# A decoder layer in split float32: two activation tiles start 224 bytes further on

## The chip, the core and the metric

One core of one Trainium2 chip runs the whole layer as one program. The metric is the device time of that program in microseconds (us), the median of the runs shown. Lower is better. Engines are named as in the profile: PE (TensorE, matmul), PEld (its weight loads), DVE (VectorE), ACT (ScalarE), POOL (GpSimd), SP (SyncE, which issues nearly all DMAs here).

## The reference, cut to what matters

The layer works on 256 tokens of width 2048, all float32, batch 1:

```
x = x + 0.5 * swiglu(rms_norm(x), ffn1)                 # 2048 -> 5632 (gate, up) -> 2048
h = rms_norm(x);  proj = h @ w_in                       # 2048 -> 11776
#   dilated attention (3 groups x 4 heads of 128), differential attention (4 heads of 2 x 128), two gates
y = sigmoid(gA) * (o_dil @ w_dil) + sigmoid(gB) * (o_diff @ w_diff)
x = x + y @ w_out
x = x + 0.5 * swiglu(rms_norm(x), ffn2)
```

Per-head norms of queries and keys, a partial rotary embedding and the softmaxes stand between; nearly all arithmetic is in the products with the weight matrices.

## The kernel before, in words

**A product in three parts.** Each weight matrix is read once, 512 columns (a chunk) by 256 rows (a group, two k tiles) at a time. `weight_groups` loads a group into `raw` (4 buffers), ACT rounds it into `w_hi` (line 94, float32r), DVE writes the rest `w_lo = raw - w_hi` (line 95); both have 3 buffers. The activations were split the same way into a high and a low tile, feature on the partitions: `xh`/`xl` for the input of the feed-forwards and of `w_in`, `ah`/`al` for the hidden layer, `oa_h`/`oa_l` and `ob_h`/`ob_l` for the two attention outputs, `yh`/`yl` for the input of `w_out`. `linear` then issues three matmuls per k tile and token tile, 12 per group:

```
nc.tensor.matmul(ps[t], xh[:, k, sl], hi[:, kk], start=k == 0, stop=False)       # line 110
nc.tensor.matmul(ps[t], xh[:, k, sl], lo[:, kk], start=False, stop=False)        # line 111
nc.tensor.matmul(ps[t], xl[:, k, sl], hi[:, kk], start=False, stop=k == nk - 1)  # line 112
```

The activation block of 128 x 128 is the operand that is loaded into the array (stationary), the 512 weight columns are streamed (moving). The names `xh, xl` inside `linear` are its parameters; the profile shows the tile that was passed.

**Stages.** First feed-forward (gate and up chunks in turn with `xh`/`xl`, then the down product with `ah`/`al`), the mixer (`w_in` with `xh`/`xl`, attention heads in between), four rounds of a gate chunk (`xh`/`xl`), a dilated branch chunk (`oa_h`/`oa_l`, 24 matmuls) and a differential branch chunk (`ob_h`/`ob_l`, 48 matmuls), then `w_out` (`yh`/`yl`), and the second feed-forward as the first. `xh`/`xl` serve 6432 of the 9216 big matmuls: 2144 on each of the three lines.

**Transposes through DRAM.** The hidden layer comes out with tokens on the partitions. `turn_blocks` transposes 32 x 32 blocks on DVE (line 154), writes them to DRAM (`blocks`, line 156) and reads them back in place (`moved`, line 159), both on SP's queue. `split_blocks` makes `ah`/`al` of it (lines 127 and 128), emitted 8 groups later (`BLOCK_WAIT`), so that PE has matrix products in front of it. ACT and DVE work in order: while ACT waits for `moved`, the next `w_hi` behind it waits too.

**Order.** The order on each engine was set when the program was built, by a scheduler; on the chip each engine keeps it and waits on semaphores. `masks` (line 282) builds the attention masks from an index table `DI` that POOL writes with an iota (line 286), and a helper table `DM`; `rsqrt_mean` (line 121) runs a power on POOL for each norm. `junk` is a work tile of one buffer that takes results which nobody reads.

**Where the tiles lie.** The built program places them at these byte addresses of a partition; the last column is the address modulo 512. Inside every one of these tiles the operands of a matmul start at multiples of 512 bytes from the tile's start.

| tile | start, before | modulo 512 |
|---|---|---|
| xh, xl | 33472, 49856 | 192 |
| w_hi (3 buffers) | 94112, 98208, 102304 | 416 |
| w_lo (3 buffers) | 106400, 110496, 114592 | 416 |
| ah, al | 120736, 165792 | 416 |
| oa_h, oa_l, ob_h, ob_l | 120736 to 137120 | 416 |
| yh, yl | 145312, 161696 | 416 |
| ident; xs | 32896; 16512 | 128 |
| dk, dq, dv, at | 161696 to 192416 | 416 |
| fq, fk, fv | 204768 to 221152 | 480 |

Of the kernel before, what the change touches and what calls it, by code (L numbers as in the profile page):

```python
# [11 lines left out]
F32 = mybir.dt.float32  # L12
F32R = mybir.dt.float32r
I32 = mybir.dt.int32
# [5 lines left out]
P = 128  # L20
NT = 2            # token tiles
S = P * NT
# [3 lines left out]
KF = FF // P  # L26
CH = 512          # columns of one weight chunk
BLOCK_WAIT = 8    # weight groups a transpose through DRAM is given
GRP = 2           # k tiles of one weight load and split
DIL_G, DIL_H = 3, 4  # L30
# [9 lines left out]
    '0x1.fa8b84p-14', '0x1.be2188p-15', '0x1.88ec22p-16', '0x1.5a0f4ep-17', '0x1.30c94ep-18')]  # L40
# 2*pi in parts whose products with a turn count below 2**19 are exact
TWO_PI = (6.25, 17.0 / 512.0, -19.0 * 2.0 ** -20)
# [5 lines left out]
def hybrid_layer_kernel(ctx: ExitStack, tc: tile.TileContext, a: dict, out: bass.AP):  # L48
# [11 lines left out]

# [1 line left out]
    # Work that hangs on ACT and DVE is emitted some weight groups later, so that the tensor engine has  # L62
    # matrix products in front of it while it waits.
    groups = 0
# [17 lines left out]
    def weight_groups(w, n0, nk):  # L82
        """Weight columns n0..n0+CH, GRP k tiles at a time, as exact float32r parts."""
        nonlocal last_hi, last_lo
        for k0 in range(0, nk, GRP):
            raw = wraw.tile([P, GRP, CH], F32, name="raw")
            hi = wspl.tile([P, GRP, CH], F32R, name="w_hi")
            lo = wspl.tile([P, GRP, CH], F32R, name="w_lo")
            step = 1 if groups == 0 else GRP
            for g in range(0, GRP, step):  # L90
                ks = slice(g, g + step)
                nc.sync.dma_start(raw[:, ks], w[(k0 + g) * P:(k0 + g + step) * P, n0:n0 + CH]
                                  .rearrange("(k p) n -> p k n", p=P))
                last_hi = nc.scalar.activation(hi[:, ks], raw[:, ks], AF.Copy)  # L94
                last_lo = nc.vector.tensor_tensor(lo[:, ks], raw[:, ks], hi[:, ks].bitcast(F32), op=ALU.subtract)  # L95
            yield k0, hi, lo

    def linear(w, n0, xh, xl, nk, ahead=None):
        """x @ w[:, n0:n0+CH] for both token tiles, left in PSUM."""
        ps = [ps_mm.tile([P, CH], F32, name="mm") for _ in range(NT)]  # L100
# [15 lines left out]
    def rsqrt_mean(ss, n, cols):  # L116
        """(ss / n + eps) ** -0.5 on [P, cols]"""
        v = small.tile([P, cols], F32, name=f"rv{cols}")
# [5 lines left out]
    def split(hi, lo, src, gain=None):  # L124
        """hi + lo = src (times a per-partition gain)"""
        if gain is None:
# [6 lines left out]
    def to_kmajor(srcs, xh, xl, k0, gains=None):  # L133
        """srcs: per token tile [P, m * 2 * P]; fills xh/xl[:, k0:k0+2*m, :] with the split transpose."""
        for h in range(srcs[0].shape[-1] // (2 * P)):
# [12 lines left out]
    def turn_blocks(srcs, pool, x=None):  # L148
        """The transpose of srcs (per token tile [P, CH]) without the tensor engine: blocks of 32 x 32
        on DVE, then a trip through DRAM that brings the blocks to their partitions.  # L150
        Block row a holds tokens 32 a + j, feature 128 kt + 4 i + q goes to partition 4 i + q of k tile kt."""
        r = pool.tile([P, 4, NT, 4, 32], F32, name="turned")               # (a i) | q t kt j
        for t in range(NT):
            nc.vector.transpose(r[:, :, t], srcs[t].rearrange("p (kt i q) -> p q kt i", i=32, q=4))  # L154
        d = dram.tile([4, P, NT * P], F32, name="blocks")                  # a | (i q) | t kt j
        nc.sync.dma_start(d.rearrange("a (i q) x -> (a i) q x", q=4), r.rearrange("p q t kt j -> p q (t kt j)"))
        if x is None:
            x = pool.tile([P, 4, NT, 4, 32], F32, name="moved")            # (i q) | a t kt j
        nc.sync.dma_start(x.rearrange("p a t kt j -> p a (t kt j)"), d.rearrange("a p x -> p a x"))
        return x  # L160

    def split_blocks(x, xh, xl, k0, gains=None):
        """xh/xl[:, k0:k0+4, :] from turn_blocks"""
        for t in range(NT):
# [16 lines left out]

# [1 line left out]
    xs = const.tile([P, NT, D], F32, name="xs")           # residual stream, tokens on partitions  # L183
    xv = a["x"][0].rearrange("(t p) d -> p t d", p=P)
# [4 lines left out]
    table = const.tile([P, 1], F32, name="table")  # L189
    nc.scalar.activation(table, mhalf[:, :1], AF.Silu)    # loads the table of the feed-forward  # L190

    def gain_columns(names, name):
        """Gains as columns of [P, number of 128-blocks]"""
        n = sum(a[k].shape[1] for k in names) // P
# [11 lines left out]

    xh = const.tile([P, KD, S], F32R, name="xh")          # feature-major operand of the linear layers
    xl = const.tile([P, KD, S], F32R, name="xl")
    g1 = gain_columns(["ffn1_norm"], "g1")

    def load_x(i):
        """256 columns of x, and their transpose"""
        if i < KD // 2:
# [37 lines left out]
    def residual(n, ps, scale, gains, ss, pool):  # L251
        """x += scale * ps on columns of chunk n; starts the next norm."""
        cols = slice(n * CH, (n + 1) * CH)
# [18 lines left out]

# [1 line left out]
    H = ROPE // 2  # L274
# [7 lines left out]
    def masks():  # L282
        # masks: 0 where a key counts, NEG elsewhere; queries of the second token tile, keys 0..255
        # (its second half is also the mask of the first tile's own keys)
        di = const.tile([P, P], I32, name="DI")                # query - key inside a tile
        nc.gpsimd.iota(di, pattern=[[-1, P]], base=0, channel_multiplier=1)
        nc.vector.tensor_scalar(mask[:, 0, P:], di, 0.0, None, op0=ALU.is_lt)
        nc.vector.tensor_scalar(mask[:, 0, :P], di, 0.0, None, op0=ALU.is_gt)
        dm = const.tile([P, P], I32, name="DM")
        for g, r in ((1, 4), (2, 16)):  # L290
# [7 lines left out]
    def rotary():  # L298
        # rotary tables, per token: [cos | cos] and [-sin | sin]
        pos = const.tile([P, NT], I32, name="pos")  # L300
# [29 lines left out]
    def head_gains():  # L330
        # q/k gains on every partition, and lambda
        for i, n in enumerate(("dil_q_norm", "dil_k_norm", "diff_q_norm", "diff_k_norm")):
# [11 lines left out]

# [1 line left out]
    later_gains = []  # L346
# [9 lines left out]
    def pinned(fn):  # L356
        """fn, behind the splits traced so far on ACT and DVE"""
        with tc.issue_after(last_hi.ins), tc.issue_after(last_lo.ins):
            fn()
# [7 lines left out]

# [1 line left out]
    rstd = []  # L369
# [10 lines left out]

    # outputs of the two branches, feature-major
    oa_h = midc.tile([P, DIL_H, S], F32R, name="oa_h")
# [3 lines left out]

    def qk_chunk(c0, gain, dst, is_key):
        """Four heads of w_in columns c0..: norm, rotary, transposed into dst
        (queries: heads, tokens; keys: as turn_blocks leaves them)."""
        ps = linear(w_in, c0, xh, xl, KD)  # L390
# [38 lines left out]
    def all_keys(k, c, h, nt):  # L429
        """Keys of head h of chunk c in nt token tiles, as a moving operand"""  # L430
        return k[:, c, :, :nt, h].rearrange("p a t j -> p t a j")

    def keys_out(ps):
        """ps [P, keys], in the shape of all_keys"""
        return ps.rearrange("p (t a j) -> p t a j", a=4, j=32)
# [8 lines left out]

# [1 line left out]
    fpool = tc.tile_pool(name="fpool", bufs=1, side="right")  # L446
# [9 lines left out]
    def diff_head(h):  # L456
        """Stages of one head, each waiting for the one before on ACT and DVE."""
        prs = []
# [65 lines left out]

# [1 line left out]
    dpool = tc.tile_pool(name="dpool", bufs=1)  # L526
# [11 lines left out]
    def dil_head(h):  # L538
        """The three groups of one matched head share one softmax: the mix by denominators."""
        prs = []  # L540
# [49 lines left out]

# [1 line left out]
    gpool = tc.tile_pool(name="gpool", bufs=1, side="right")  # L592
# [9 lines left out]

# [1 line left out]
    ypool = tc.tile_pool(name="ypool", bufs=1)  # L604
# [48 lines left out]

# [1 line left out]
    ov = out[0].rearrange("(t p) d -> t p d", p=P)  # L655
# [37 lines left out]
```

## Time and profile before

| what | value |
|---|---|
| time, median of 3 runs | 2204.64 us (2200.27 to 2207.46) |
| profiled execution, span | 2206.8 us |
| PE busy | 2183.6 us, 99% |
| DVE busy | 1217.6 us, 55% |
| ACT busy | 994.8 us, 45% |
| DMA | 452.04 MB, mean 205 GB/s, main queue 65.3% of 16 engines |
| mean granted clock of TensorE | 0.999 |

The page gives the profiled execution by its span alone, from its first to its last instruction; no time around it is listed. A matmul's duration in the profile is from its start to its modelled end, and matmuls overlap: the next starts before the last one's end. What a matmul costs PE is therefore the step from its start to the next one's start, and durations serve only to compare one group with another.

### The profile page before, as it was taken

To read this page: it belongs to the slowest core of one execution; us is meant where nothing else is said; L and a number is where in the kernel's file an instruction comes from. 1 tells how busy PE (TensorE), PEld (TensorE's weight loads), DVE (VectorE), ACT (ScalarE), POOL (GpSimd) and SP (SyncE) were. 2 spreads that over 40 slices of the span, in tenths; PEclk is the share of its full clock that TensorE was granted. 3 is DMA by queue.
4 is the path that set the end of the run, shared out by engine and by line. 5 is a ranking of instruction groups with operands and counts; after the bars stand their busy time and mean duration, and the time that the engine had idled before them with its cause. 6 is when DMAs were issued, how large, how long until landed. Compare 5 with 4: busy or idle time off the path is not lost.

```text
span 2206.8 us, 24998 instructions
## 1 busy us (share of the span) xinstructions
PE 2183.6 (99%) x9490; PEld 1767.1 (80%) x9490; DVE 1217.6 (55%) x1440; ACT 994.8 (45%) x1193; POOL 41.9 (2%) x41
## 2 busy tenths in 40 slices
PE   9999999999999999999999999999999999999999
PEld 7777787888888877887778888887887878778887
DVE  5645555555555566766565556565555555554444
ACT  5434444443444445555445444454444444343333
POOL 0000000000000010101100000000000000000000
PEclk9999999999999999999999999999999999999999
DMA  7666666676666666666665676666666766666664
GB/s 230 213 211 205 208 204 213 213 211 209 212 207 204 196 194 199 208 211 209 200 191 153 183 226 209 219 212 202 208 213 208 217 205 205 220 209 207 202 202 143
DMA packets 241437, 452.04 MB, mean 205 GB/s; under 512 B 14322, under 2 KB 38436, under 8 KB 241316
## 3 DMA queue, kind: packets, MB, share of 16 engines
q1 hardware_dynamic: 239792, 449.89, 65.3%
q8 instruction: 74, 1.21, 0.2%
q10 hardware_dynamic: 1524, 0.55, 0.1%
q14 instruction: 47, 0.39, 0.1%
HBM read 426.80 MB, written 23.59 MB: 204 GB/s over the span
## 4 chain that ended last, share of the span: by engine, by line
PE 82%; DMA 8%; DVE 5%; ACT 2%; issue 2%; POOL 1%; ACTq 0%; SPq 0%; DVEq 0%; POOLq 0%
PE mm L111 27%; PE mm L112 27%; PE mm L110 26%; DMA blocks<-turned 3%; DMA moved<-blocks 3%; DVE w_lo L95 3%; ACT w_hi L94 2%; DVE turned L154 1%; POOL rr L121 1%; DMA q<-blocks 1%; DVE q L404 0%; DMA raw<-in_ffn_w_gate_dram 0%; DMA dk<-blocks 0%; PE s L549 0%; DMA junk<-in_diff_lk_dram 0%
## 5 line engine op out<-in xcount | busy, mean ns | idle before, releaser
L95 DVE TENSOR_TENSOR w_lo<-raw,w_hi 128x1024 fp32r<-128x1024 f32 (+1 forms) x769 | 933.4, 1220 | 826.0 <-ACT w_hi L94 825.5
L94 ACT ACTIVATE w_hi<-raw 128x1024 fp32r<-128x1024 f32 (+1 forms) x769 | 808.5, 1057 | 978.5 <-PE mm L112 955.3
L111 PE MATMUL mm<-w_lo,xh 128*128 128x512 f32 x2144 | 855.4, 399 | 7.3 <-DVE w_lo L95 7.1
L112 PE MATMUL mm<-w_hi,xl 128*128 128x512 f32 x2144 | 846.9, 396 | 0.2
L110 PE MATMUL mm<-w_hi,xh 128*128 128x512 f32 x2144 | 771.7, 397 | 0.0
L111 PEld LDWEIGHTS mm<-w_lo,xh 128*128 128x128 f32 x2144 | 403.7, 188 | 109.0 <-DVE w_lo L95 14.1
L110 PEld LDWEIGHTS mm<-w_hi,xh 128*128 128x128 f32 x2144 | 403.2, 188 | 97.1 <-ACT w_hi L94 0.4
L112 PEld LDWEIGHTS mm<-w_hi,xl 128*128 128x128 f32 x2144 | 404.0, 189 | 95.3 <-DVE xl L131 1.1
L111 PE MATMUL mm<-w_lo,ah 128*128 128x512 f32 x704 | 274.5, 390 | 2.1 <-DVE w_lo L95 2.1
L112 PE MATMUL mm<-w_hi,al 128*128 128x512 f32 x704 | 274.1, 389 | 0.0
L110 PE MATMUL mm<-w_hi,ah 128*128 128x512 f32 x704 | 245.9, 390 | 0.5 <-ACT w_hi L94 0.5
L111 PEld LDWEIGHTS mm<-w_lo,ah 128*128 128x128 f32 x704 | 132.1, 188 | 31.3 <-DVE w_lo L95 3.9
L110 PEld LDWEIGHTS mm<-w_hi,ah 128*128 128x128 f32 x704 | 131.9, 188 | 29.3 <-ACT w_hi L94 2.0
L112 PEld LDWEIGHTS mm<-w_hi,al 128*128 128x128 f32 x704 | 132.2, 188 | 27.1
L128 DVE TENSOR_TENSOR al<-moved,ah 128x512 fp32r<-128x512 f32 x44 | 28.5, 689 | 75.4 <-ACT ah L127 75.4
L121 POOL TENSOR_TENSOR rr<-rv,mhalf 128x4 f32<-128x4 f32 (+1 forms) x34 | 41.0, 1211 | 1427.7 <-DVE rv L119 1427.6
L127 ACT ACTIVATE ah<-moved 128x512 fp32r<-128x512 f32 x44 | 25.4, 624 | 88.9 <-DMA moved<-blocks 88.9
L111 PE MATMUL mm<-w_lo,yh 128*128 128x512 f32 x128 | 50.2, 392 | 0.5 <-DVE w_lo L95 0.5
L112 PE MATMUL mm<-w_hi,yl 128*128 128x512 f32 x128 | 49.9, 390 | 0.0
L154 DVE STREAM_TRANSPOSE turned<-sg 128x512 f32<-128x512 f32 x44 | 48.6, 1106 | 0.0
L110 PE MATMUL mm<-w_hi,yh 128*128 128x512 f32 x128 | 44.9, 390 | 0.2 <-ACT w_hi L94 0.2
L240 ACT ACTIVATE sg<-mm,rr 128x512 f32<-128x512 f32 x44 | 30.0, 688 | 23.0 <-PE mm L112 22.7
(142 smaller groups left out, 734.5 us busy)
## 6 DMA issues: line engine op xcount, KB each, us to landing
raw<-in_w_in_dram SPq DMA_DIRECT2D x184, 512.0 KB, 3.8
raw<-in_ffn_w_up_dram SPq DMA_DIRECT2D x176, 512.0 KB, 4.3
raw<-in_ffn_w_down_dram SPq DMA_DIRECT2D x176, 512.0 KB, 4.4
raw<-in_ffn_w_gate_dram SPq DMA_DIRECT2D x175, 512.0 KB, 4.3
blocks<-turned SPq DMA_DIRECT2D x41, 512.0 KB, 4.3
raw<-in_w_out_dram SPq DMA_DIRECT2D x32, 512.0 KB, 4.7
moved<-blocks SPq DMA_DIRECT2D x31, 512.0 KB, 4.8
raw<-in_w_diff_branch_dram SPq DMA_DIRECT2D x16, 512.0 KB, 4.3
```

The source lines that it names most:

```text
L94: last_hi = nc.scalar.activation(hi[:, ks], raw[:, ks], AF.Copy)
L95: last_lo = nc.vector.tensor_tensor(lo[:, ks], raw[:, ks], hi[:, ks].bitcast(F32), op=ALU.subtract)
L110: nc.tensor.matmul(ps[t], xh[:, k, sl], hi[:, kk], start=k == 0, stop=False)
L111: nc.tensor.matmul(ps[t], xh[:, k, sl], lo[:, kk], start=False, stop=False)
L112: nc.tensor.matmul(ps[t], xl[:, k, sl], hi[:, kk], start=False, stop=k == nk - 1)
L121: nc.gpsimd.tensor_tensor(r, v, mhalf[:, :cols], op=ALU.pow)
L127: nc.scalar.activation(hi, src, AF.Copy)
L128: nc.vector.tensor_tensor(lo, src, hi.bitcast(F32), op=ALU.subtract)
L154: nc.vector.transpose(r[:, :, t], srcs[t].rearrange("p (kt i q) -> p q kt i", i=32, q=4))
L240: nc.scalar.activation(s, ps[t], AF.Silu, scale=rs[t])
```

## The change

`xh` gets 56 elements (224 bytes) in front, and `xl` 72 elements (288 bytes) behind, so that together they are 512 bytes longer. In the built program `xh` starts at 33472 as before and its first used byte is at 33696; `xl` is at 50080. Both are 416 modulo 512. The two tables `DI` and `DM` of `masks` (512 bytes each) give up places of their own and become halves of a `junk` tile. Everything that is allocated behind them (the weights, `ah`, `yh` and so on) moves down by 512 bytes, and so keeps its place modulo 512; the `f` tiles and `sig`, placed from the other end, do not move.

```
+LEAD = 56
...
-    xh = const.tile([P, KD, S], F32R, name="xh")          # feature-major operand of the linear layers
-    xl = const.tile([P, KD, S], F32R, name="xl")
+    xh = const.tile([P, LEAD + KD * S], F32R, name="xh")[:, LEAD:].rearrange("p (k s) -> p k s", s=S)
+    xl = const.tile([P, KD * S + P - LEAD], F32R, name="xl")[:, :KD * S].rearrange("p (k s) -> p k s", s=S)
...
-        di = const.tile([P, P], I32, name="DI")                # query - key inside a tile
+        both = work.tile([P, 2, P], I32, name="junk")
+        di, dm = both[:, 0], both[:, 1]
...
-        dm = const.tile([P, P], I32, name="DM")
```

The rest of the diff takes comments out; three lines more stand before the functions, so a line number of the kernel before is 1 to 4 smaller than the same line's afterwards.

The order of the instructions on PE, ACT and SP is the same in both programs, waits included; on DVE only the names `DI` and `DM` become `junk`. On POOL one instruction moves. In the program before, the iota of `masks` (`DI`) stands between the two instructions that make the identity matrix, ahead of the first norm's two powers (`rr`):

```order
masks.py:197 MEMSET ident 128x128
L286 ISA
L286 IOTA DI 128x128
masks.py:199 AFFINE_SELECT ident<-ident 128x128
L121 TENSOR_TENSOR rr_369<-rv_367,mhalf 128x1
L121 TENSOR_TENSOR rr_375<-rv_373,mhalf 128x1
```

In the changed program the same stretch of POOL reads:

```order
masks.py:197 MEMSET ident 128x128
masks.py:199 ISA
masks.py:199 AFFINE_SELECT ident<-ident 128x128
L122 TENSOR_TENSOR rr_369<-rv_367,mhalf 128x1
L290 IOTA junk 128x128
L122 TENSOR_TENSOR rr_375<-rv_373,mhalf 128x1
```

The iota now stands between the two powers of the first norm, and it waits for ACT, which uses `junk` for the squares of that norm.

## Rows read from the trace of the kernel before

**Rows 1.** The page, share of the span: busy us, instructions.
```profile
PE 2183.6 (99%) x9490; PEld 1767.1 (80%) x9490; DVE 1217.6 (55%) x1440; ACT 994.8 (45%) x1193; POOL 41.9 (2%) x41
```
**Rows 2.** The page's groups: line, engine, names, shape, count | busy, mean ns | idle before.
```profile
L111 PE MATMUL mm<-w_lo,xh 128*128 128x512 f32 x2144 | 855.4, 399 | 7.3 <-DVE w_lo L95 7.1
...
L111 PE MATMUL mm<-w_lo,ah 128*128 128x512 f32 x704 | 274.5, 390 | 2.1 <-DVE w_lo L95 2.1
```
**Rows 3.** Groups of PE from 1196 to 1362 us, where the tiles alternate.
```profile
L111 PE MATMUL mm<-w_lo,xh 128*128 128x512 f32 x157 | 62.6, 399 | 0.0
...
L111 PE MATMUL mm<-w_lo,ob_h 128*128 128x512 f32 x48 | 18.7, 389 | 0.0
```
**Rows 4.** Timeline of PE at 1244 and 1260 us: start, duration, instruction.
```profile
1244.05 0.62 PE L110 MATMUL mm<-w_hi,oa_h 128*128 128x512 f32 x2
...
1260.14 0.40 PE L112 MATMUL mm<-w_hi,ob_l 128*128 128x512 f32 x1
1260.38 0.62 PE L110 MATMUL mm<-w_hi,xh 128*128 128x512 f32 x2
```
**Rows 5.** Timeline of ACT from 238 to 262 us, first feed-forward.
```profile
239.18 1.06 ACT L94 ACTIVATE w_hi<-raw 128x1024 fp32r<-128x1024 f32 x1 [1.74 <-PE mm L112]
...
250.38 1.06 ACT L94 ACTIVATE w_hi<-raw 128x1024 fp32r<-128x1024 f32 x1 [1.74 <-PE mm L112]
255.97 1.15 ACT L127 ACTIVATE ah<-moved 128x512 fp32r<-128x512 f32 x2 [4.53 <-DMA moved<-blocks]
```
**Rows 6.** Timeline of ACT from 560 to 575 us, down product.
```profile
561.85 1.06 ACT L94 ACTIVATE w_hi<-raw 128x1024 fp32r<-128x1024 f32 x1 [1.66 <-PE mm L112]
...
572.72 1.07 ACT L94 ACTIVATE w_hi<-raw 128x1024 fp32r<-128x1024 f32 x1 [1.66 <-PE mm L112]
```
**Rows 7.** Groups of PE over the span: plain float32 products of the attention.
```profile
L578 PE MATMUL tr<-at,dv 128*128 128x256 f32 x24 | 7.1, 378 | 0.0
...
L502 PE MATMUL s<-fv,at 128*128 128x256 f32 x24 | 6.5, 378 | 0.0
```
**Rows 8.** PE from 0 to 36 us: us, PE busy (x), granted clock, DMA share, GB/s.
```profile
0.00:36.00 36.00, 30.86 (x138) 1.00 0.79 255
```
**Rows 9.** Timeline of DVE: the chunk's product is ready.
```profile
241.42 1.41 DVE L244 SCALAR_TENSOR_TENSOR sg<-mm,rr,sg 128x512 f32<-128x512 f32 x2
```
**Rows 10.** Timeline of PE from 256 to 262 us.
```profile
259.39 0.50 PE L111 MATMUL mm<-w_lo,xh 128*128 128x512 f32 x1 [0.17 <-DVE w_lo L95]
```
**Rows 11.** Waits of ACT over the span: us in total, times, longest.
```profile
ACT ah L127 <- DMA moved<-blocks: 88.9, 22, 4.9
```
**Rows 12.** Timeline of ACT: the split with a short wait at 300 us.
```profile
299.91 1.16 ACT L127 ACTIVATE ah<-moved 128x512 fp32r<-128x512 f32 x2 [3.22 <-DMA moved<-blocks]
```
**Rows 13.** Waits of PE from 760 to 1240 us, the mixer.
```profile
PE mm L111 <- DVE w_lo L95: 2.2, 4, 0.8
PE s L549 <- DMA dk<-blocks: 2.0, 2, 1.0
```
**Rows 14.** Timeline of PE from 135 to 143 us, behind its longest wait.
```profile
139.48 0.80 PE L111 MATMUL mm<-w_lo,xh 128*128 128x512 f32 x1 [3.44 <-DVE w_lo L95]
140.08 0.63 PE L112 MATMUL mm<-w_hi,xl 128*128 128x512 f32 x1
140.50 0.63 PE L111 MATMUL mm<-w_lo,xh 128*128 128x512 f32 x1
```
**Rows 15.** Stretch behind that wait: us, PE busy (x), granted clock, DMA share, GB/s.
```profile
139.90:142.20 2.30, 2.30 (x6) 0.50 0.63 170
```
**Rows 16.** Timeline of ACT, then of POOL, at the first norm.
```profile
34.56 0.18 ACT L175 ACTIVATION_READ_ACCUMULATOR junk<-xs 128x1 f32 x1
...
39.47 0.69 ACT L240 ACTIVATE sg<-mm,rr 128x512 f32<-128x512 f32 x1 [2.97 <-PE mm L112]
...
35.21 0.55 POOL L121 TENSOR_TENSOR rr<-rv,mhalf 128x1 f32<-128x1 f32 x1 [0.20 <-DVE rv L119]
```
**Rows 17.** The page, DMA rate in 40 slices of the span, GB/s.
```profile
GB/s 230 213 211 205 208 204 213 213 211 209 212 207 204 196 194 199 208 211 209 200 191 153 183 226 209 219 212 202 208 213 208 217 205 205 220 209 207 202 202 143
```

## The prediction

> **What bounds the kernel now.** I read the page's shares first: PE is busy 99% of the span and DVE 55%, ACT 45% [rows 1]. So the time is the number of matmuls times the step from one start to the next, plus a little waiting, and a change to where operands lie can only matter through that step.
>
> Next I read the groups by tile. All big matmuls have one shape, 128 x 128 by 512 columns, and yet the ones on `xh` last 399 ns and the ones on `ah` 390 ns [rows 2]. That could be the stage. The stretch from 1196 to 1362 us rules this out: there gate chunks (`xh`) and branch chunks (`ob_h`) alternate every 16 to 20 us, with the same ACT, DVE and DMA work around them, and the means are still 399 and 389 ns [rows 3].
>
> Durations overlap, so the price is the step, taken from starts. From the first `oa_h` matmul at 1244.05 to the first `xh` matmul at 1260.38 [rows 4] stand the 24 + 48 = 72 matmuls of two branch chunks: 16.33 / 72 = 226.8 ns each. For `xh` ACT's timeline gives it, because ACT starts one `w_hi` per group of 12 matmuls as PE frees a buffer: 239.18 to 250.38 is four groups, 11.20 / 48 = 233.3 ns [rows 5]. In the down product, on `ah`, four groups take 561.85 to 572.72: 10.87 / 48 = 226.5 ns [rows 6], which agrees with 226.8. So a matmul on `xh`/`xl` costs 6.5 ns more than the same one on any other activation tile. In the table of addresses these tiles differ in one respect that holds for every group: `xh`/`xl` start at 192 modulo 512, all others, and the weights they meet, at 416.
>
> One detail points to the meeting of the stationary load and the moving stream: the last `ob_l` matmul before a gate chunk, which streams while an `xh` block is loaded for the next one, already lasts 0.40 us and steps 0.24 us [rows 4], against 389 ns in its group [rows 3].
>
> **The change, part by part.** *The move of `xh`/`xl`.* It makes 192 into 416, the residue at which 226.8 ns is measured. 6432 matmuls x 6.5 ns = 41.8 us. The first 36 us do not follow PE: it is busy for 30.86 of them only, waiting on first loads and their splits [rows 8]. About 100 of its matmuls therefore gain nothing, 0.7 us. Gross gain: 41.1 us, all of it on the path, since PE never has another engine in front of it for long.
>
> *What is late next.* The transposes through DRAM take fixed time, while the matrix work that covers them shrinks. One chain in rows: the chunk's product is complete at 241.42 [rows 9], ACT reaches the split of `moved` after its `w_hi` at 250.38 and waits 4.53 us until 255.97 [rows 5], the next `w_hi` and `w_lo` stand behind it, and PE gets them at 259.39, 0.17 us late [rows 10]. The cover from 241.42 to 259.39 less that wait is 17.8 us, 6.4 groups of 2.80 us [rows 5]. A group becomes 12 x 226.8 = 2.72 us, so the cover shrinks by 6.4 x 0.078 = 0.5 us. Each chain that is late now gives back 0.5 us; one that has slack less. ACT's waits for `moved` are 22, 88.9 us in all, 4.04 us on average [rows 11]. A wait of 3.22 us leaves PE without a gap [rows 12], one of 4.53 us does not [rows 5]; I put the border at 4.1 us, close to the mean, so about half of the 22 are late. The last chain of each feed-forward is covered by `ah` matmuls, whose step does not change; ten late ones are left: 10 x 0.5 = 5.0 us. The others lie up to 0.9 us under the border; some four of them cross it by a little, 0.5 us together. The mixer has six such waits of PE [rows 13], on the same kind of chain; with 0.5 us each, and one more that crosses, 3.5 us. PE's longest wait, 3.44 us at 139.48 [rows 14], hangs on a load of fixed length and grows by some 0.2 us. Given back: 9.2 us.
>
> The bounds of this term: nothing, if the DRAM trips land earlier by chance, and 0.5 us for each of some 22 chains in the feed-forwards and 20 in the mixer, 21 us, if all were at the border. I take 9.2, the count of those that the rows show late.
>
> *The supply.* Weights come per group, so the rate must rise by 2.8% in the `xh` stages. The page shows 204 to 213 GB/s there and 226 and 230 in single slices [rows 17]; 213 x 1.028 = 219 lies below these. I take nothing, up to 5 us if it doesn't hold.
>
> *The iota.* It moves behind ACT's last square of the first norm, which ends at 34.74, and ahead of the second power, which starts at 35.21 [rows 16]. Even if it held that power back by 0.3 us, the first reader, `sg`, starts at 39.47, and waits for PE, not for the power [rows 16]. Cost: nothing; the cover is 3.7 us. `DI` and `DM` in `junk` add no wait to DVE's or ACT's instructions. The writers of `xh`/`xl` on ACT and DVE write to 416 instead of 192, as they write `ah` now; nothing.
>
> **Sum.** 41.1 - 9.2 = 31.9 us. The profiled span becomes 2206.8 - 31.9 = 2174.9 us. The span is 2.2 us over the median of the runs, inside their range of 2200.3 to 2207.5, so I subtract the same from the median: 2204.64 - 31.9 = 2172.7, say 2173 us.
>
> [...]
>
> **The rivals.**
>
> *Half the effect.* Only some of the three lines gain, for example because where `xl` or `w_lo` lies counts in another way than the residue. For it: the rows show each line's excess, but not which of the two operands' places makes it. Against it: four groups of `w_hi` take in all three lines alike, and on `ah` they come out at 226.5 ns [rows 6], with no line left behind. Half of 41.8 is 20.9, less 4.6 given back: 2204.6 - 16.3 = 2188 us.
>
> *Place, not residue.* `xh`/`xl` are the only operands below 66 KB; all others lie above 94 KB. If the region costs the 6.5 ns, 224 bytes change nothing. For it: the plain float32 products with operands 64 bytes apart modulo 512 (`fv` with `at`) last 378 ns, as those that lie alike (`at` with `dv`) [rows 7], so a difference in residue alone does not slow every matmul. Against it: these stream only 256 columns in that time, at half the rate; and `ah`, which reaches over 90 KB, shows no gradient. 2204.6 us, no change.
>
> [...]
>
> **How the numbers follow.** Forecast 0.78, half the effect 0.08, no effect 0.11, slower 0.03. The forecast's own range is 2204.6 - 41.8 = 2163 (nothing given back) to 2163 + 21 = 2184 (all chains late). With 2 us below for the spread of the runs, and above up to the half effect's 2188, the range is 2161 to 2188; it leaves out no effect, slower, and a few hundredths at the edges. No change means within 0.3%, 6.6 us, about what a measurement of this kernel can tell. Faster: 0.78 + 0.08 = 0.86; same 0.11; slower 0.03.
>
> **What would show it.** Right: the mean of the `xh` and `xl` groups falls from 396 to 399 ns to 389 or 390, `w_hi` starts every 2.72 us in the gate and up chunks, the groups on `ah`, `ob_h`, `yh` stay. The share given back shows in ACT's waits for `moved`: their mean rises from 4.04 by about 0.4 us, and more of PE's gaps name `w_lo`. Wrong: durations on `xh` near 396 ns with the address moved (place, not residue); one of the three lines unchanged (half the effect); a fall of the step without a fall of the time, which would put the DRAM trips or the loads in PE's place.

## The result, and the profile after

The changed kernel takes 2175.26 us (median of 4 runs, 2172.41 to 2175.95) against 2205.47 us for the kernel before beside it (median of 4, 2200.27 to 2207.46). The ratio is 0.9859, 95% interval 0.9843 to 0.9874: 1.4% faster, 30 us. The forecast was 2173 us. The profiled span went from 2206.8 to 2173.1 us, 33.7 us.

The page's shares, which answer to [rows 1]: PE still fills the span.

```profile
PE 2148.0 (99%) x9490; PEld 1765.7 (81%) x9490; DVE 1216.5 (56%) x1440; ACT 994.6 (46%) x1193; POOL 45.1 (2%) x41
```

The groups of PE by tile (line, names, count | busy, mean ns | idle before), which answer to [rows 2]. Lines are numbered one higher than before.

```profile
L112 PE MATMUL mm<-w_lo,xh 128*128 128x512 f32 x2144 | 843.1, 393 | 8.4 <-DVE w_lo L96 7.9
L113 PE MATMUL mm<-w_hi,xl 128*128 128x512 f32 x2144 | 834.5, 390 | 0.1
L111 PE MATMUL mm<-w_hi,xh 128*128 128x512 f32 x2144 | 759.3, 392 | 0.1
L112 PE MATMUL mm<-w_lo,ah 128*128 128x512 f32 x704 | 274.5, 390 | 2.6 <-DVE w_lo L96 2.6
```

The group on `xh` came down from 399 to 393 ns; the one on `ah` did not move. The remaining difference of 2 to 3 ns is in the means alone: the median is 389 ns on every tile, and the means on `xh`/`xl` hold some matmuls at half clock (12 of 0.63 us or more, at a granted clock of 0.50), behind a wait, or directly behind a short attention product (67 of over 0.45 us). In the alternating stretch (1179 to 1341 us here), which answers to [rows 3], the first group is `xh` and the second `ob_h`; nine `xh`/`xl` matmuls of 0.47 to 0.59 us, eight of them behind such a product, make the difference:

```profile
L112 PE MATMUL mm<-w_lo,xh 128*128 128x512 f32 x156 | 61.3, 393 | 0.1
...
L112 PE MATMUL mm<-w_lo,ob_h 128*128 128x512 f32 x48 | 18.7, 389 | 0.0
```

ACT's timeline shows the step itself, as in [rows 5]:

```profile
235.25 1.06 ACT L95 ACTIVATE w_hi<-raw 128x1024 fp32r<-128x1024 f32 x1 [1.66 <-PE mm L113]
...
246.13 1.06 ACT L95 ACTIVATE w_hi<-raw 128x1024 fp32r<-128x1024 f32 x1 [1.66 <-PE mm L113]
...
253.70 1.15 ACT L128 ACTIVATE ah<-moved 128x512 fp32r<-128x512 f32 x2 [3.79 <-DMA moved<-blocks]
```

Four groups take 10.88 us: 2.72 us each, 226.7 ns a matmul, where it was 233.3. The waits that answer to [rows 11] and [rows 13] (ACT over the span, then PE in the mixer):

```profile
ACT ah L128 <- DMA moved<-blocks: 86.4, 22, 5.0
```
```profile
PE mm L112 <- DVE w_lo L96: 2.2, 3, 0.8
PE s L552 <- DMA dk<-blocks: 2.0, 2, 1.0
PE s L471 <- issue: 1.2, 1, 1.2
```

For a full account I took all starts of the 9490 matmuls. Steps up to 260 ns on `xh`/`xl` have a mean of 233.3 ns before and 227.1 after, on about 6300 matmuls: 39 us. Longer steps (called gaps from here on), each less 230 ns, sum to 33.4 us before and 38.1 after: 4.7 us given back. 39 - 4.7 = 34 us, the fall of the span.

### The profile page after: what moved, and what is told of

Its sections match the earlier page's. It is cut to its first block, busy times and chain, and to the rows that moved or that the text cites. A ratio compares the mean times of both kernels' runs of the same rounds, so it can differ in the third digit from the quotient of the medians.

```text
span 2173.1 us, 24998 instructions
## 1 busy us (share of the span) xinstructions
PE 2148.0 (99%) x9490; PEld 1765.7 (81%) x9490; DVE 1216.5 (56%) x1440; ACT 994.6 (46%) x1193; POOL 45.1 (2%) x41
## 4 chain that ended last, share of the span: by engine, by line
PE 79%; DMA 10%; DVE 6%; ACT 2%; issue 2%; POOL 1%; SPq 0%; ACTq 0%; DVEq 0%; POOLq 0%
PE mm L112 26%; PE mm L113 26%; PE mm L111 26%; DMA moved<-blocks 4%; DMA blocks<-turned 4%; DVE w_lo L96 3%; ACT w_hi L95 2%; DVE turned L155 1%; POOL rr L122 1%; DMA q<-blocks 1%; DMA raw<-in_w_out_dram 1%; DMA raw<-in_ffn_w_up_dram 0%; DVE q L407 0%; PE s L552 0%; DMA dk<-blocks 0%
## 5 line engine op out<-in xcount | busy, mean ns | idle before, releaser
L112 PE MATMUL mm<-w_lo,xh 128*128 128x512 f32 x2144 | 843.1, 393 | 8.4 <-DVE w_lo L96 7.9
L113 PE MATMUL mm<-w_hi,xl 128*128 128x512 f32 x2144 | 834.5, 390 | 0.1
L111 PE MATMUL mm<-w_hi,xh 128*128 128x512 f32 x2144 | 759.3, 392 | 0.1
L128 ACT ACTIVATE ah<-moved 128x512 fp32r<-128x512 f32 x44 | 25.4, 624 | 86.4 <-DMA moved<-blocks 86.4
L155 DVE STREAM_TRANSPOSE turned<-sg 128x512 f32<-128x512 f32 x44 | 48.4, 1100 | 0.0
```

What stands on the lines that cost most here:

```text
L128: nc.scalar.activation(hi, src, AF.Copy)
```

## The experiments

All were timed beside the kernel before in three comparisons, e1 to e4 (its median 2211.1 us), e5 to e8 (2211.8) and e9 to e12 (2209.0); the changed kernel's own result is a fourth (2205.5). Across them the ratio to before is compared, not the time. "Step" is the mean start-to-start time of the matmuls on `xh`/`xl`, gaps over 260 ns left out, and "distance" is where the weights start minus where `xh`/`xl` start, modulo 512.

| run | xh/xl, weights modulo 512 | distance | step, ns | ratio to before (95%) |
|---|---|---|---|---|
| before | 192, 416 | 224 | 233.3 | 1 |
| changed | 416, 416 | 0 | 227.1 | 0.9859 (0.9843 to 0.9874) |
| e1 | 192, 416 | 224 | 233.3 | 0.9996 (0.9985 to 1.0007) |
| e2 | 192, 192 | 0 | 227.1 | 0.9884 (0.9867 to 0.9900) |
| e3 | 352, 416 | 64 | 229.3 | 0.9914 (0.9899 to 0.9929) |
| e4 | 160, 416 | 256 | 227.1 | 0.9873 (0.9856 to 0.9890) |
| e5 | 288, 416 | 128 | 232.6 | 0.9982 (0.9973 to 0.9992) |
| e6 | 384, 416 | 32 | 233.3 | 0.9997 (0.9983 to 1.0011) |
| e7 | xh 192, xl 416, weights 416 | 224 and 0 | 232.6 | 0.9983 (0.9965 to 1.0001) |

**e1, the lead taken away.**

```
-LEAD = 56
+LEAD = 0
```

> The changed kernel with the lead of xh set from 56 elements to 0: xh and xl start at 192 modulo 512 again, the weights and all else stay at 416, and the tables of the masks stay in junk. Theory (the residue of xh/xl against the weights costs the 6.5 ns): the step on xh is 233 ns again, groups on xh last 396 to 399 ns, time 2205 us. Rival (the iota and the tables made the difference, or the first 512 bytes freed): steps of 227 ns stay, time 2175 us.

Measured: 2210.43 us, 0.9996 of before. Its group on `xh`:

```profile
L112 PE MATMUL mm<-w_lo,xh 128*128 128x512 f32 x2144 | 854.0, 399 | 7.6 <-DVE w_lo L96 7.6
```

399 ns, as before the change, with the iota and the tables left where the change put them. Those parts are worth nothing that this can tell; all of the gain is in the 224 bytes.

**e2, everything at 192.**

```
-LEAD = 56
+LEAD = 0
...
     neg_lam = const.tile([P, 1], F32, name="neg_lam")
+    const.tile([P, 72], F32, name="pad")
```

> As the run before it (xh/xl at 192), with 288 bytes of padding at the end of the constants, so that the weights, ah, al, oa, ob, yh, yl also start at 192 modulo 512. Theory (alike is what counts, not 416): steps of 227 ns on xh and on ah, time 2175 us. Rival one (192 itself is a bad residue): 233 ns on all 9216 matmuls, 6.5 ns x 9216 = 60 us over 2175, 2235 us. Rival two (the place below 66 KB is bad): 233 ns on xh, 227 on the others, 2205 us.

Measured: 2186.48 us, 0.9884.

```profile
L112 PE MATMUL mm<-w_lo,xh 128*128 128x512 f32 x2144 | 843.6, 394 | 14.5 <-DVE w_lo L96 14.0
...
L112 PE MATMUL mm<-w_lo,ah 128*128 128x512 f32 x704 | 274.4, 390 | 1.9 <-DVE w_lo L96 1.9
```

`xh` at its old address, below 66 KB and at residue 192, runs at the short step once the weights lie alike. So neither the place nor the residue by itself costs anything: both rivals fall. It came out 11 us over the 2175 that was expected. Some 6 us of that lie in the comparison, whose kernel before took 2211.1 us against 2205.5 beside the changed kernel. In the profiles the step is the same (227.1 ns) and the gaps are larger, 51.4 us against 38.1; PE's idle time before `w_lo` is 14.0 us here against 7.9 in the changed kernel. e9 shows larger gaps for the unaltered changed kernel too.

**e3 and e4, 64 and 256 bytes apart.** `LEAD` is 40 and 120.

> The lead of xh is 40 elements: xh and xl at 352 modulo 512, 64 bytes before the weights' 416. Theory in the strict form (any difference modulo 512 costs the same): step 233 ns, 2205 us. Graded form (a price that grows with the distance, 224 bytes costs 6.5 ns): about 2 ns, 2184 us. Rival (only residues modulo 64 count): 0 ns, 2175 us.

> The lead of xh is 120 elements: xh and xl at 160 modulo 512, 256 bytes from the weights' 416, so alike modulo 256 but not modulo 512. Theory in the strict form (modulo 512): step 233 ns, 2205 us. Rival (the period is 256, 128 or 64 bytes): 227 ns, 2175 us. Graded form: 233 to 235 ns, 2205 to 2215 us.

Measured: e3 2192.34 us, 0.9914; e4 2182.63 us, 0.9873. The groups on `xh`, e3 and then e4:

```profile
L112 PE MATMUL mm<-w_lo,xh 128*128 128x512 f32 x2144 | 848.7, 396 | 9.2 <-DVE w_lo L96 8.6
```
```profile
L112 PE MATMUL mm<-w_lo,xh 128*128 128x512 f32 x2144 | 843.0, 393 | 13.8 <-DVE w_lo L96 13.5
```

At 256 bytes the step is as short as at 0, against the theory as I had put it: alike modulo 256 is enough. At 64 bytes it is 229.3 ns, a third of the excess; the strict form and the rival modulo 64 both fall, the graded form had the right size.

**e5 and e6, 128 and 32 bytes apart.** `LEAD` is 24 and 48.

> The lead of xh is 24 elements: xh and xl at 288 modulo 512, 128 bytes before the weights' 416. So far 0 and 256 bytes apart step 227 ns, 64 bytes 229 to 230, and 224 (which is 32 on the other side, modulo 256) 233. Theory (the period is 256 bytes): not 227 but between 228 and 234 ns, a time 5 to 45 us over the changed kernel's. Rival (the period is 128 bytes): 227 ns, the changed kernel's time.

> The lead of xh is 48 elements: xh and xl at 384 modulo 512, 32 bytes before the weights; before the change they were 32 bytes after them modulo 256. Theory one (only the distance counts, not its sign): 233 ns, the time of before. Theory two (the side counts, because the load begins a little after the stream): a step other than 233, at 227 to 231 ns, and a time 0 to 25 us over the changed kernel's.

Measured: e5 2208.76 us, 0.9982; e6 2211.36 us, 0.9997. Groups of e5 and e6:

```profile
L112 PE MATMUL mm<-w_lo,xh 128*128 128x512 f32 x2144 | 853.8, 398 | 8.4 <-DVE w_lo L96 8.4
```
```profile
L112 PE MATMUL mm<-w_lo,xh 128*128 128x512 f32 x2144 | 853.3, 398 | 6.1 <-DVE w_lo L96 6.1
```

The period is not 128 bytes: at 128 the step is 232.6 ns. Of the distances tried, only 0 and 256 are free. At 32 it costs the same on either side (233.3 ns; 224 is 32 the other way, modulo 256), so the sign does not count there. In the profile of before the load of a block does start a little after the stream: 97% of the loads start 2 to 4 ns after the matmul that streams meanwhile. The price does not grow with the distance either: 233.3 at 32, 229.3 at 64, 232.6 at 128. I have no model for that order.

**e7, `xl` alone alike.**

```
-    xh = const.tile([P, LEAD + KD * S], F32R, name="xh")[:, LEAD:].rearrange("p (k s) -> p k s", s=S)
-    xl = const.tile([P, KD * S + P - LEAD], F32R, name="xl")[:, :KD * S].rearrange("p (k s) -> p k s", s=S)
+    xh = const.tile([P, KD * S], F32R, name="xh").rearrange("p (k s) -> p k s", s=S)
+    xl = const.tile([P, KD * S + P], F32R, name="xl")[:, LEAD:LEAD + KD * S].rearrange("p (k s) -> p k s", s=S)
```

> xh at 192 modulo 512 as before the change, xl and the weights at 416. PE runs the lines in the order hi with xh, lo with xh, hi with xl, and the block of the next matmul is loaded while one streams. Theory one (the price falls on the matmul that streams while a misplaced block is loaded): line 113 (hi, xl), behind which xh is loaded, steps 233 ns, line 112 (lo, xh), behind which xl is loaded, 227 ns. Theory two (it falls on the matmul whose own block is misplaced): lines 111 and 112 at 233, line 113 at 227. Time in both: a third of the effect gone, 12 to 14 us under before.

Measured: 2205.75 us, 0.9983, interval up to 1.0001. A third of the blocks lies alike, and next to nothing is gained. The three groups:

```profile
L112 PE MATMUL mm<-w_lo,xh 128*128 128x512 f32 x2144 | 848.5, 396 | 9.9 <-DVE w_lo L96 9.6
L113 PE MATMUL mm<-w_hi,xl 128*128 128x512 f32 x2144 | 848.2, 397 | 0.1
L111 PE MATMUL mm<-w_hi,xh 128*128 128x512 f32 x2144 | 768.6, 396 | 0.3 <-ACT w_hi L95 0.3
```

Steps by line, from the starts: 232.4 on line 111, 230.9 on line 112, 234.6 on line 113. Theory two falls: line 113, whose own block lies alike, is the longest. Theory one has the order of lines 112 and 113 right, but line 112 should have been at 227. (PE's order is less regular than the expectation says, but line 112 is always followed by an `xl` block, and lines 111 and 113 by an `xh` block.) Sorted by the matmuls before and after as well, the steps run from 229.3 ns (line 112 between two on `xl`) to 237.5 (line 113 between two of line 112). A block that lies alike does not free its matmul while its neighbours do not. Which of the three (block in use, block being loaded, stream) meets which, and where, stays open.

**e8 and e10, the late transposes taken out, with and without the move.** e8 is the changed kernel, e10 the same with `LEAD = 0`:

```
-                defer(BLOCK_WAIT, lambda x=x, j=j: split_blocks(x, ah, al, 4 * j))
+                defer(BLOCK_WAIT, lambda x=x, j=j: pinned(lambda: split_blocks(x, ah, al, 4 * j)))
...
-            defer(BLOCK_WAIT, lambda: split_blocks(x, xh, xl, 4 * n, gains))
+            defer(BLOCK_WAIT, lambda: pinned(lambda: split_blocks(x, xh, xl, 4 * n, gains)))
```

`pinned` holds the split behind the weight splits that stand before it in the code. Without it the scheduler had put the split two groups earlier than `BLOCK_WAIT` asks for.

> The changed kernel with every split of a transpose through DRAM (feed-forwards and residuals) held behind the weight splits traced so far, which puts it two groups, 5.4 us, further back on ACT and DVE. Theory (these chains give back about 9 us of the move's gain and some 6 us more were late before): ACT's waits for moved fall under the 4.1 us at which PE sees them, and the time falls by 8 to 12 us under the changed kernel. Rival (the waits are covered or come back elsewhere): within 2 us of it.

> The held-back splits of e8 with the lead of xh at 0, so that xh/xl lie at 192 again. Between it and e8 stands the move alone, without late transposes. Theory (the move is worth about 40 us gross, of which late chains give back 4 to 9): e8 under e10 by 39 to 42 us, against 30 to 33 us between the changed kernel and before. Rival (the gross gain is itself nearer 31 us): the same 31 us here.

Measured: e8 2166.60 us, 0.9799 (0.9777 to 0.9822); e10 2199.46 us, 0.9954 (0.9940 to 0.9968). In e8 ACT finds `moved` landed when it comes to the split, with no idle time before it, and the next `w_hi` waits for PE again:

```profile
71.50 1.14 ACT L128 ACTIVATE ah<-moved 128x512 fp32r<-128x512 f32 x2
73.25 1.06 ACT L95 ACTIVATE w_hi<-raw 128x1024 fp32r<-128x1024 f32 x1 [0.62 <-PE mm L113]
```

The chains were late: holding them back is worth 0.6% between the changed kernel and e8, and 0.5% between before and e10 (13 us and 10 us). The first of these sets two comparisons against each other, and the changed kernel's second one, e9 below, would make it 1.0%. But they were about as late before the move: the gaps fall by 8.9 us with the move (38.1 to 29.2) and by 8.6 without it (33.4 to 24.8), where e8's expectation has them grow by 9 us through the move. The other half of the theory failed too. The move is worth 34 us here (0.9954 to 0.9799), not 39 to 42. The two ratios come from different comparisons, and their intervals allow some 6 us either way; the profiled spans lie 34.8 us apart. The step falls by the full 6.2 ns (233.3 to 227.1), 39 us, but the gaps rise from 24.8 to 29.2 us although the transposes of the feed-forwards are covered: the mixer, whose transposes were not held back, takes 489.9 us in e10 and 483.8 in e8, 6 us less, where its 20 chunks of 96 matmuls would give 12.

**e9, the changed kernel once more.**

> The changed kernel itself, beside the next three on one chip: 0.984 to 0.988 of before. It gives the measure for them.

Measured: 2185.68 us, 0.9896 (0.9879 to 0.9913), outside the expectation and 0.4% above the first comparison. The step is the same, 227.2 ns, and so is the program. What I see to differ are the trips through DRAM. Issue to landing (KB each, median us), e9 and then the changed kernel's first profile:

```profile
moved<-blocks SPq DMA_DIRECT2D x31, 512.0 KB, 5.3
```
```profile
moved<-blocks SPq DMA_DIRECT2D x31, 512.0 KB, 4.5
```

and with it the wait of ACT for it in e9:

```profile
ACT ah L128 <- DMA moved<-blocks: 97.1, 22, 5.5
```

Its gaps sum to 49.2 us, 11 more than in the first profile. By the medians the move gained 23.4 us in this comparison and 30.2 in the first, so it gave back some 7 us more here; the kernel before has no profile in this comparison that would say where. What made the trips longer I did not find out.

**e11, `ah`/`al` moved away.**

```
-            ah = apool.tile([P, KF, S], F32R, name="ah")
+            ah = apool.tile([P, 72 + KF * S], F32R, name="ah")[:, 72:].rearrange("p (k s) -> p k s", s=S)
```

> The changed kernel with ah and al moved from 416 to 192 modulo 512 (288 bytes in front of ah), everything else as it is. Theory (any activation tile that is not alike with the weights pays): the step on ah goes from 226.8 to 233.3 ns, 2112 x 6.5 = 13.7 us over the changed kernel; steps on xh stay at 227. Rival (only the tiles below 66 KB pay): no change.

Measured: 2199.08 us, 0.9950 (0.9934 to 0.9967), 13.4 us over e9 beside it. The groups:

```profile
L112 PE MATMUL mm<-w_lo,xh 128*128 128x512 f32 x2144 | 843.9, 394 | 11.9 <-DVE w_lo L96 11.4
...
L112 PE MATMUL mm<-w_lo,ah 128*128 128x512 f32 x704 | 278.8, 396 | 1.0 <-DVE w_lo L96 1.0
```

The step on `ah`/`al` is 233.3 ns now, on `xh`/`xl` still 227.1. The price goes with the relation to the weights, whichever tile has it: 2112 x 6.5 = 13.7 us was expected.

**e12, the best version: e8, and the loads for lambda ahead of their use.**

```
-    defer(44, lambda: pinned(head_gains))
+    defer(40, lambda: pinned(load_lambda))
+    defer(45, lambda: pinned(head_gains))
+    defer(50, lambda: pinned(load_gains))
```

(`load_lambda` and `load_gains` hold the eight DMAs that stood at the head of `head_gains`.)

> e8, and the loads for lambda issued five groups ahead of their arithmetic on DVE instead of directly before it; the loads of the q/k gains come after it. PE's longest wait, some 3.4 us plus about ten matmuls at half clock, goes: 5 to 6 us under e8 if nothing else comes in its place, within 1 us of e8 if the issue of the loads on ACT's queue (which held up w_hi for 4.5 us) is what counts.

Measured: 2160.42 us, 0.9779 (0.9763 to 0.9794), 25 us or 1.2% under the changed kernel beside it. In the changed kernel PE's longest wait and its aftermath read as follows, the wait in PE's timeline, and then the stretch behind it (us, PE busy, granted clock, DMA share, GB/s), as in [rows 14, 15]:

```profile
139.41 0.79 PE L112 MATMUL mm<-w_lo,xh 128*128 128x512 f32 x1 [3.48 <-DVE w_lo L96]
```
```profile
139.90:144.60 4.70, 4.70 (x12) 0.50 0.80 241
```

In e12 no wait of PE is left between 36 and 528 us. The loads are issued at 113.95 to 115.76 and DVE's arithmetic on them starts at 129.72, without a wait between two weight splits:

```profile
115.31 0.45 ACTq L343 DMA_DIRECT2D junk<-in_diff_lk_dram  x1
```
```profile
128.57 1.23 DVE L96 TENSOR_TENSOR w_lo<-raw,w_hi 128x1024 fp32r<-128x1024 f32 x1 [1.49 <-ACT w_hi L95]
129.72 0.49 DVE L349 TENSOR_TENSOR junk<-junk 128x128 f32<-128x128 f32 x2
```

The spans of e8 and e12, 2163.2 and 2157.9 us, lie 5.3 us apart, as expected; they come from different comparisons, though, and by the ratios the difference is 0.2%, and the intervals overlap.

## Why the prediction was right, step by step

*The cause.* Right: the residue of the stationary tile against the weights. e1 (undone alone), e2 (all moved together) and e11 (another tile made to pay) show it. The reading that carried it was the alternation of `xh` and `ob_h` in one stretch [rows 3], since it took stage, clock and neighbours out of the comparison. It could not tell the residue from the region below 66 KB; e2 could. A meeting with ACT's or DVE's own accesses is no rival: 559 of the steps on `xh`/`xl` before fall into time in which neither engine was busy, and their mean is 233 ns too.

*The period.* 512 bytes, the form in which the change is described, is more than is needed. e4 shows that 256 does.

*The meeting of load and stream.* Only argued, and no more than half borne out. The single place that was read for it [rows 4] is typical: in the trace of before PE goes over from an aligned tile (one that starts alike with the weights) to `xh` five times, and the last aligned matmul steps 235 ns each time, where 226.8 is the mean on such tiles. But at the six places where it goes back, the last matmul on `xh`/`xl`, while an aligned block is loaded for the next one, still steps 232 or 233 ns, and the aligned one after it 231. So the price does not sit on the load of a misaligned block alone, as e7 says too. With the same instructions the step is 227.1 or 233.3 ns by the address of the stationary tile against the weights (the changed kernel and e1). What in PE loses the time, no run shows.

*The gross gain.* Forecast 41.1 us, measured 39: the long step was right, and the short one came out at 227.1 on average instead of 226.8.

*What is late next.* The mechanism is there, but the sum put it in the wrong places, and one profile does not show its size. Forecast 9.2 us: 5.5 from the chains of the feed-forwards, 3.5 from the mixer, 0.2 from the longest wait. The first comparison gave 4.7 us. PE's lost time behind the 22 splits of the feed-forwards (steps over 240 ns in the 8 us behind each, less 230 ns) was 6.0 us before and 7.0 after, so the chains gave back 1.0 us of it; the mixer gave back 0.9; and the half clock behind the longest wait (granted 0.50, steps of 0.43 us) lasted 12 matmuls instead of 6, which is 1.2 us that the forecast had not counted. The rest is spread over other stages. The read-back landed sooner in that profile (`moved` 4.5 us from issue to landing, 4.8 before), so ACT's waits did not rise from 4.04 us on average, as the prediction had said, but fell to 86.4 / 22 = 3.93. What did move is the border: before, a wait of 3.91 us at 1930 us left PE without a gap, and now one of 3.95 us at 1547 us was followed by a gap of 0.10 us.

In e9 the same program behaves as forecast and more: the waits average 97.1 / 22 = 4.41 us, 0.37 up, and PE's lost time behind the 22 splits is 14.3 us. The first comparison was a lucky one. In the five profiles in which `xh`/`xl` step 227 ns and nothing is held back (changed, e2, e4, e9, e11) the gaps sum to 38.1, 51.4, 48.4, 49.2 and 47.1 us; in the five with steps of 232.6 or 233.3 ns (before, e1, e5, e6, e7) to 33.4, 31.1, 37.8, 30.5 and 34.5. That is 13 us given back on average, more than forecast. The read-back takes 4.9 to 5.3 us in four of the first five and 4.5 to 4.8 in the others; whether the shorter step itself makes it longer was not tested.

e8 and e10 settle that the chains were late and cost PE some 9 us. They do not settle that the move's 4.7 us came from them: with these chains held back (but for three waits on `yh`, none is left in ACT's waits) the move still gives back 4.4 us, 3.8 of them in the mixer, close to the 3.5 that were forecast there.

*The supply and the iota.* Right: ACT's waits for `raw` sum to 2.7 us as before. A late load that kept ACT waiting for 4 to 5 us turned up in some other profiles, in e9 (4.3 us) but also at the long step, in e5, e6 and e10 (5.0, 4.5 and 4.4 us), so the shorter step is not needed for it. e1 shows that the iota and the tables cost nothing. The iota runs at 35.66 and the second power follows at 35.90; its reader comes at 39.97 and waits for PE:

```profile
35.66 0.24 POOL L290 IOTA junk<- 128x128 int32 x1
35.90 0.56 POOL L122 TENSOR_TENSOR rr<-rv,mhalf 128x1 f32<-128x1 f32 x1
```
```profile
39.97 1.27 ACT L243 ACTIVATE sg<-mm,rr 128x512 f32<-128x512 f32 x2 [2.85 <-PE mm L113]
```

*The sum.* 2173 against 2175.3 us is closer than its terms deserve: on the spans, the gain was forecast at 41.1 - 9.2 = 31.9 and came as 39 - 4.7 = 34; on the medians it was 30.2. Errors of 2 and 4.5 us in the two terms went against each other, and the small give-back was luck: by the ratio of e9 the same kernel would have come out at 2182 us, still inside the range of 2161 to 2188. The chance of 0.03 for slower was an estimate; the highest ratio to before of any run is 0.9997 (e6).

## What to carry to other kernels

Where PE is the bound and equal matmuls differ by a few ns from tile to tile, compare them in a stretch in which the tiles alternate, and look at where the tiles start modulo 256 bytes against the streamed operand: the step was 227.1 ns at distances of 0 and 256 bytes, and 229.3 to 233.3 at 32, 64, 128 and 224. A lead of a few dozen elements per tile was worth 1.0 to 1.4% here. Only this one shape and type was measured (float32r, 128 x 128 against 512 columns, a new block for every matmul). Take the step from starts, not from durations, and price beside the gain what the shorter cover does to every chain that does not shrink with it (here the read-back: 4.8 us before, 4.5 and 5.3 with the shorter step). A chain that a scheduler has placed needs a look at its order: a wait constant in the code need not be the wait on the chip.

## What the runs showed that I had not expected

- The excess is not monotone in the distance: 233.3 ns at 32 bytes, 229.3 at 64, 232.6 at 128, 227.1 at 0 and 256 (e3 to e6).
- Aligning one of two stationary tiles that alternate gives almost nothing: 232.6 ns on average, and the matmuls on the aligned one are the longest, 234.6 ns (e7).
- The same program can differ by 0.4% in its ratio to before from one comparison to another (0.9859 and 0.9896), while the step stays at 227 ns. The difference is in PE's gaps, and the read-back took 4.5 us in one profile and 5.3 in the other; that the DRAM trips are the reason is only argued.
- After PE's wait of 3.48 us its granted clock was 0.50 for some 5 us, 12 matmuls or so; in the profile of before, behind one of 3.44 us, it lasted about half as long [rows 14, 15]. Over the 13 profiles with this wait, of 3.1 to 4.0 us, 6 to 12 matmuls lasted 0.63 us or more in ten, where 0.39 to 0.40 is usual, and none did in three (e1, e3 and e7).
